# Order edges for three mixer steps, and two squares from GpSimd to VectorE, in a two-layer hybrid encoder

## The chip, the cores and the metric

The kernel runs on one core of a Trainium2 chip. The core has five engines that work side by side, each through its own queue of instructions in a fixed order: TensorE (PE, matrix multiplications and transposes), VectorE (DVE), ScalarE (ACT), GpSimd (POOL) and SyncE (SP, which starts most DMA transfers). The metric is the time of one execution on the device, in microseconds (us).

## The reference, cut to what matters

Two layers of an encoder run over 512 tokens of width 1024, in fp32, and a last RMSNorm follows. One layer:

```
xn = RMSNorm(x);  h = xn @ W_in
A: gated DeltaNet, both directions (short convolution over 5 tokens on q, k, v;
   per chunk the inverse of a unit triangular matrix; scan over the chunks)
B: differential attention (two softmax maps per head, rotary)
C: attention in a window of +-128 tokens, grouped heads (rotary)
D: mLSTM, both directions (decay and input gates, running maximum)
x = x + (sum_b sigmoid(xn @ W_gate_b) * (mixer_b @ W_branch_b)) @ W_out
x = x + relu(RMSNorm(x) @ W1)^2 @ W2
```

The convolution of mixer A is `silu(centred_dwconv(qkv, conv_w))`. The output of mixer D is, per head, `num / max(|den|, exp(-m))`, summed over the two directions, then normed per head and gated.

## The kernel before

**Dense work.** A large matmul in fp32 is made of three passes in the faster fp32r format. Weight and activation are each split into a high and a low half (`wh`, `wl`; `xh`, `xl`), and high x high, low x high and high x low are summed in PSUM. The weight split is in `emit_split`: ACT copies the raw fp32 weight to `wh` (L312), DVE subtracts `wh` from it to give `wl` (L313), in two pieces for each load. Raw weights lie in two buffers (`wr`), the halves in three each. The dense matmuls form a list of items, in the order of the string `ORDER` (Aq, Ak, Av: the columns of mixer A; z, do: gates; dv, dqk: columns of D; B, C: columns of B and C) and after them branch projections, merge, output projection and MLP. An item asks for its weights with `get`, which first traces the splits up to one load ahead (two in the MLP) and the DMA some loads ahead.

**Mixers.** The mixers are generators. Each step that is traced ends with a `yield` of some nanoseconds, and `fill` then traces dense steps of about 1300 ns each until this time is paid. So dense work and mixer work are traced interleaved. The code does not fix the order on an engine: a planner puts the traced instructions into each engine's queue, by when it reckons them ready and by the order in which they were traced. An instruction traced later may so run earlier.

**The places that the change touches.**
- Mixer A, `group` (L1267 on): for each pair of heads and half of the chunks the matrix `tt_` is computed (L1287 to L1289), rounded to fp16 (`th`, L1291) and transposed on PE (L1298). DVE multiplies the transposes with a sign mask to give `D` (L1300), and POOL makes `Y` in the same way (L1301). Six levels follow that double the block size of the inverse; each begins with `th` x `D` on PE (L1311). There are 16 D in the run, in pairs.
- Mixer A, `conv`: ACT copies a PSUM bank to `ci` (L978) and scales it (L980), DVE adds the four other taps (L982), ACT and DVE finish with L984 and L986.
- Mixer D, `hout(h)`: for each of four token tiles PE sums both directions (L1475). ACT and DVE compute the denominators (L1477 to L1479). ACT scales one direction into `ho` (L1481), DVE adds the other (L1482). After the last head `head_norm` squares on POOL (L1153), sums on DVE (L1155), takes the root (L247, L248) and multiplies (L1157, L1158); PE then transposes the result (L1164).
- Mixer B, `put_k`: after the rotary product (L1028 to L1031, the last on POOL) two pieces of a key are cast on ACT (L1045, L1046), their low halves taken on DVE (L1047) and copied (L1048).
- MLP, `m1_evac(fg, j)`: for the first group of the hidden layer ACT takes the ReLU of a PSUM bank (L785) and squares it to `hh` (L786), POOL squares it again in fp32 (L787), DVE subtracts to get `hl` (L788). It runs for j = 0 to 3 in each layer. In the groups after it POOL also adds weight blocks for a seven-product scheme (L833), and PE multiplies with the splits of these (L856 to L858).

Of the kernel before, what the change touches and what calls it, by code (L numbers as in the profile page):

```python
# [13 lines left out]
AF = mybir.ActivationFunctionType  # L14
ALU = mybir.AluOpType
# [3 lines left out]
S = 512  # L19
# [96 lines left out]
def encoder(ctx: ExitStack, tc: tile.TileContext, a: dict, out: bass.AP, dbg: dict = None):  # L116
    nc = tc.nc
    dbg = dbg or {}
    pe, dve, act, pool = nc.tensor, nc.vector, nc.scalar, nc.gpsimd
    mm = pe.matmul  # L120
    cp = ctx.enter_context(tc.tile_pool(name="cp", bufs=1))
    lp = ctx.enter_context(tc.tile_pool(name="lp", bufs=1))
    wp = ctx.enter_context(tc.tile_pool(name="wp", bufs=3))
# [10 lines left out]
    def nm(s):  # L134
        cnt[0] += 1
        return f"{s}_{cnt[0]}"
# [11 lines left out]
    def A(dt=F32, s="t", w=S):  # L148
        o = place(s)
        return ar.tile([P, 576], dt, tag="ar", name=nm(s))[:, o:o + w]  # L150

    def AH(s="h"):
        t = ar.tile([P, 1152], F16, tag="ar", name=nm(s))[:, 2 * place(s):]
        return t[:, :S], t[:, S:2 * S]
# [5 lines left out]
    def B4(dt=F32, s="b", off=None):  # L160
        return B(dt, s, off=off).rearrange("p (k c) -> p k c", k=4)
# [4 lines left out]
    def PSM(dt=F32):  # L166
        return pm.tile([P, S], dt, tag="pm", name=nm("pm"))

    def SM(w, tag):
        return sp.tile([P, w], F32, tag=tag, name=nm(tag))  # L170

    def f(ap):
        return ap.bitcast(F32)

    v4 = lambda ap: ap.rearrange("p (d h c) -> p d h c", d=2, h=2)
# [7 lines left out]
    def bmid(ap2, n):  # L183
        sh = list(ap2.shape)
        return ap2.unsqueeze(1).to_broadcast([sh[0], n] + sh[1:])

    def rev(ap, r):
        return ap[:, ::-1] if r else ap
# [113 lines left out]
    def emit_split(i):  # L302
        w = loads[i]
        raw = w["src"]() if "src" in w else raws.pop(i)
        if "dest" in w:
            wh, wl = w["dest"]()
        else:
            wh = wp.tile([P, w["kt"], w["nc"]], F32R, tag="wh", name=nm("wh"))
            wl = wp.tile([P, w["kt"], w["nc"]], F32R, tag="wl", name=nm("wl"))
        n = w["kt"] // G["sp"]  # L310
        for k in range(0, w["kt"], n):
            act.copy(wh[:, k:k + n], raw[:, k:k + n])  # L312
            dve.tensor_tensor(wl[:, k:k + n], raw[:, k:k + n], f(wh[:, k:k + n]), op=ALU.subtract)  # L313
        wt[i] = (wh, wl)

    def step():
# [227 lines left out]
    def build(l, L):  # L544
# [234 lines left out]
        def m1_evac(fg, j):  # L779
            def ev(ps):  # L780
                if j == 0:
                    L.h[fg] = (B4(F32R, "hh"), B4(F32R, "hl"))
                hh, hl = L.h[fg]
                r, q = A(s="r"), A(s="r2")
                act.activation(r, ps, AF.Relu)  # L785
                act.activation(hh[:, j, :], r, AF.Square)  # L786
                pool.tensor_tensor(q, r, r, op=ALU.mult)  # L787
                dve.tensor_tensor(hl[:, j, :], q, f(hh[:, j, :]), op=ALU.subtract)  # L788
            return ev

# [175 lines left out]
    def conv(L, kind, h, ps):  # L966
        if kind == "k" and h == 0:
            L.kb, L.ss = B4(s="kb"), None
        if kind == "q" and h == 0:
            L.qb = B4(s="qb")  # L970
        if kind == "v" and h == 0:
            L.vb = B4(s="vb")
        ft = {"q": 0, "k": 4, "v": 8}[kind] + h
        cw = L.cw
        ci = A(s="ci", w=S + 4)
        pool.memset(ci[:, 0:2], 0.0)
        pool.memset(ci[:, S + 2:S + 4], 0.0)
        act.copy(ci[:, 2:S + 2], ps)  # L978
        ac = A(s="ac")
        act.activation(ac, ci[:, 0:S], AF.Copy, scale=cw[:, 0, ft:ft + 1])  # L980
        for k in range(1, 5):
            dve.scalar_tensor_tensor(ac, ci[:, k:k + S], cw[:, k, ft:ft + 1], ac, op0=ALU.mult, op1=ALU.add)  # L982
        sg = A(s="sg")
        act.activation(sg, ac, AF.Tanh)  # L984
        dst = {"q": L.qb if kind == "q" else None, "k": L.kb, "v": L.vb if kind == "v" else None}[kind][:, h, :]
        dve.scalar_tensor_tensor(dst, sg, 1.0, ac, op0=ALU.add, op1=ALU.mult)  # L986
# [55 lines left out]
    def put_k(rt, dh, dl, h0, l0):  # L1042
        for e, (own, oth) in enumerate(halves):
            t, u = dh[:, h0 + e, :], dl[:, l0 + e, :]
            act.copy(t[own], rt[own])  # L1045
            act.copy(t[oth], rt[own])  # L1046
            dve.tensor_tensor(u[own], rt[own], f(t[own]), op=ALU.subtract)  # L1047
            dve.tensor_copy(u[oth], f(u[own]))  # L1048

    def b_qk(L, hp, kind, b, bank):  # L1050
        if kind == "q" and b == 0:
# [94 lines left out]
    def ynew():  # L1146
        return B4(F32R, "yh"), B4(F32R, "yl")
# [24 lines left out]
    def mixer_a(l, L):  # L1172
# [94 lines left out]
        def group(hp, first, cks, step, kk, kq):  # L1267
# [6 lines left out]
            for which in range(2):  # L1274
                r = PSM()
# [17 lines left out]
            sm = lambda lv: rev(sgn[:, lv], first).unsqueeze(2).to_broadcast([P, 2, 2, P])  # L1293
            smT = lambda lv: rev(sgn[:, lv], 1 - first).unsqueeze(2).to_broadcast([P, 2, 2, P])
            yield
            ps = PSM(F16)
            for m in range(4):
                pe.transpose(ps[:, blk(m)], th[:, blk(m)], identh)  # L1298
            D, Y = AH("DY")
            dve.tensor_tensor(v4(D), v4(ps), sm(0), op=ALU.mult)  # L1300
            pool.tensor_tensor(v4(Y), v4(th), smT(0), op=ALU.mult)  # L1301
            yield
            for lv in range(1, NLVL):
                w = 1 << lv
                hv = lambda t: t.rearrange("p (i g c) -> p i g c", i=2, c=w)
# [24 lines left out]
            q = A(s="q")  # L1330
# [130 lines left out]
    def mixer_d(l, L):  # L1461
        vx, EM, mb = L.vx, L.EM, L.mb
        qs, kh, kl = [[t[:, h, :] for h in range(4)] for t in (L.dq, L.dkh, L.dkl)]
        hsum = [A(s="hs") for _ in range(NT)]
        Ws = {}

        def hout(h):
            W = Ws.pop(h)
            for t in range(NT):
                hb = PSM()  # L1470
                hv = hb.rearrange("p (d c) -> p d c", d=2)
                for d in range(2):
                    js = range(0, t + 1) if d == 0 else range(t, NT)
                    for j in js:
                        mm(hv[:, d, 0:130], W[d][j][:, blk(t)], vx[:, j, h, :], start=(j == js[0]), stop=(j == js[-1]))  # L1475
                dn = SM(2, "dn")
                act.activation(dn, hv[:, :, 128], AF.Abs)  # L1477
                dve.tensor_tensor(dn, dn, EM[:, t, h::4], op=ALU.max)
                dve.reciprocal(dn, dn)  # L1479
                ho = hsum[t][:, blk(h)]  # L1480
                act.activation(ho, hv[:, 0, 0:128], AF.Copy, scale=dn[:, 0:1])  # L1481
                dve.scalar_tensor_tensor(ho, hv[:, 1, 0:128], dn[:, 1:2], ho, op0=ALU.mult, op1=ALU.add)  # L1482
                yield G['dh']

        for h in range(4):
            R, Rm = [], []
            for d in range(2):
                r = PSM()
                mm(r, oneh(0, d * 4 + h), L.RB1, start=True, stop=True)
                r1, r2 = A(s="R"), A(s="Rm")  # L1490
                act.copy(r1, r)
                dve.tensor_tensor(m4(r2), m4(r), bmid(f(neg[1][:, d, :]), 4), op=ALU.add)
                R.append(r1)
                Rm.append(r2)
            yield G['dr']
            W = [[None] * 4, [None] * 4]
            if h > 0:
                yield from hout(h - 1)
            for j in range(NT):
                s_ = PSM()  # L1500
                mm(s_, kh[h][:, blk(j)], qs[h], start=True, stop=False)
                mm(s_, kl[h][:, blk(j)], qs[h], start=False, stop=True)
                for d in range(2):
                    ts_ = range(j, NT) if d == 0 else range(0, j + 1)
                    n = len(ts_)
                    w_ = A(s="W") if n > 0 else None
                    for t in ts_:
                        act.activation(w_[:, blk(t)], (Rm if t == j else R)[d][:, blk(t)], AF.Exp,
                                       bias=mb[:, d, j, t, h:h + 1])
                    sl = slice(ts_[0] * P, (ts_[-1] + 1) * P)  # L1510
                    dve.tensor_tensor(w_[:, sl], s_[:, sl], w_[:, sl], op=ALU.mult)
                    W[d][j] = w_
                yield G['ds']
            Ws[h] = W
        yield G['hl']
        yield from hout(3)
        yT = ynew()
        L.y["d"] = yT
        ys = {}
        for tt in range(NT):  # L1520
            ys[tt] = head_norm(hsum[tt], 4, L.og[:, tt, :].rearrange("p (h c) -> p h c", h=4))
            dump_y(f"yd{l}", ys[tt], 4, tt, 0)
            yield G['yn']
        yield G['yw']
        for tt in range(NT):
            y_T(ys.pop(tt), 4, tt, 0, yT)
            yield G['yt']
        marks.add(f"yd{l}")
# [231 lines left out]
```

## Time and profile before

| | |
|---|---|
| three runs | 2319.26, 2322.42, 2322.50 us; median 2322.42 |
| the profiled execution | 2320.51 us, span of its instructions 2318.7 us |
| mean granted clock of TensorE | 0.995 |
| instructions in the profile | 41278 |
| DMA | 200.81 MB, mean 87 GB/s |

The span is the time from the first to the last instruction in the profile; the execution's own time lies around it. The clock is given as a share of TensorE's full speed (2.4 GHz). In the rows below, a line such as L313 is the line of the kernel that the instruction comes from, `wl<-wr,wh` says what it writes and reads, and `x2` that two instructions in a row are shown as one. Times are counted from the span's start.

### The profile page before, as it was taken

The numbers are of one execution on the slowest core, as the hardware profiler recorded it, in microseconds if no ns is written. First come the engines' busy times: TensorE is split into PE (matmuls) and PEld (weight loads), VectorE is DVE, ScalarE is ACT, GpSimd is POOL, SyncE is SP. The second block draws the span as 40 slices with busy tenths as digits, with TensorE's granted clock in tenths as the row PEclk, the third lists the DMA queues.
The fourth block names the chain that finished last, engine by engine and source line by source line (L and its number), as shares of the span: only waits on it lengthen the run. The fifth ranks groups of instructions, "written<-read, shape, count | busy, mean of one in ns | idle before, by whom it ended". The sixth has DMA issues, their size and how long they took to land.

```text
span 2318.7 us, 41278 instructions
## 1 busy us (share of the span) xinstructions
PE 2244.4 (97%) x15944; PEld 2010.0 (87%) x15944; DVE 1606.3 (69%) x2944; ACT 1236.3 (53%) x2827; POOL 772.9 (33%) x819
## 2 busy tenths in 40 slices
PE   7999999999999999999999999999999999999998
PEld 6879987878788989999987799878877889899998
DVE  5875547697886477677767755487877854867776
ACT  4565444765765264444445654366576633544443
POOL 1046552032332134443201655412313310434341
PEclk9999999999999999999999999999999999999999
DMA  6322131222122523233323122311322234233322
GB/s 154 93 54 65 56 96 57 58 91 82 52 72 82 164 67 125 92 102 117 110 78 91 55 56 65 92 56 55 100 74 64 65 112 139 87 100 110 101 83 91
DMA packets 234773, 200.81 MB, mean 87 GB/s; under 512 B 31825, under 2 KB 223697, under 8 KB 234577
## 3 DMA queue, kind: packets, MB, share of 16 engines
q1 hardware_dynamic: 231552, 193.09, 27.6%
q10 hardware_dynamic: 2304, 4.20, 0.5%
q8 instruction: 125, 2.05, 0.4%
q0 software_dynamic: 720, 0.89, 0.2%
q14 instruction: 72, 0.58, 0.1%
HBM read 190.25 MB, written 8.39 MB: 86 GB/s over the span
## 4 chain that ended last, share of the span: by engine, by line
PE 77%; DVE 7%; ACT 6%; POOL 4%; issue 3%; DMA 0%; POOLq 0%; DVEq 0%; ACTq 0%
PE pd L455 8%; PE pd L457 8%; PE pd L456 8%; PE pd L412 7%; PE pd L413 7%; PE pd L414 7%; PE pm L858 4%; PE pm L857 4%; PE pm L856 4%; PE pd L427 2%; PE pd L426 2%; PE pd L428 2%; ACT r L1028 1%; POOL r L1031 1%; DVE wl L313 1%
## 5 line engine op out<-in xcount | busy, mean ns | idle before, releaser
L313 DVE TENSOR_TENSOR wl<-wr,wh 128x512 fp32r<-128x512 f32 x540 | 413.1, 785 | 168.0 <-ACT wh L312 160.6
L312 ACT CAST wh<-wr 128x512 fp32r<-128x512 f32 x540 | 316.6, 620 | 216.0 <-PE pd L456 76.9
L455 PE MATMUL pd<-xh,wh 128*128 128x512 f32 (+1 forms) x768 | 307.5, 401 | 0.5 <-ACT xh L242 0.5
L457 PE MATMUL pd<-xh,wl 128*128 128x512 f32 (+1 forms) x768 | 298.0, 388 | 0.0
L456 PE MATMUL pd<-xl,wh 128*128 128x512 f32 (+1 forms) x768 | 296.0, 386 | 1.8 <-DVE xl L243 1.8
L414 PE MATMUL pd<-wh,hl 128*128 128x256 f32 x896 | 247.4, 276 | 0.0
L413 PE MATMUL pd<-wl,hh 128*128 128x256 f32 x896 | 247.4, 276 | 0.0
L412 PE MATMUL pd<-wh,hh 128*128 128x256 f32 x896 | 247.4, 276 | 0.0
L312 ACT CAST wh<-wq 128x512 fp32r<-128x512 f32 x196 | 115.2, 619 | 217.2 <-PE pd L414 91.5
L313 DVE TENSOR_TENSOR wl<-wq,wh 128x512 fp32r<-128x512 f32 x196 | 182.3, 964 | 12.9 <-ACT wh L312 12.8
L833 POOL TENSOR_TENSOR wq<-wq,wq 128x512 f32<-128x512 f32 x84 | 124.9, 1494 | 159.6 <-DVE wl L313 149.5
L457 PEld LDWEIGHTS pd<-xh,wl 128*128 128x128 f32 x768 | 145.9, 190 | 28.9
L456 PEld LDWEIGHTS pd<-xl,wh 128*128 128x128 f32 x768 | 146.5, 191 | 25.3 <-DVE xl L243 2.7
L412 PEld LDWEIGHTS pd<-wh,hh 128*128 128x128 f32 x896 | 168.2, 188 | 0.0
L413 PEld LDWEIGHTS pd<-wl,hh 128*128 128x128 f32 x896 | 168.2, 188 | 0.0
L414 PEld LDWEIGHTS pd<-wh,hl 128*128 128x128 f32 x896 | 168.2, 188 | 0.0
L455 PEld LDWEIGHTS pd<-xh,wh 128*128 128x128 f32 x768 | 146.2, 191 | 22.2 <-ACT xh L242 1.0
L701 DVE TENSOR_TENSOR x<-pd,x 128x512 f32<-128x512 f32 x124 | 84.8, 688 | 95.9 <-PE pd L414 95.9
L412 PE MATMUL pd<-wh,xh 128*128 128x256 f32 x512 | 150.8, 295 | 0.0
L413 PE MATMUL pd<-wl,xh 128*128 128x256 f32 x512 | 145.6, 284 | 0.0
L414 PE MATMUL pd<-wh,xl 128*128 128x256 f32 x512 | 144.7, 283 | 0.0
L1031 POOL TENSOR_TENSOR r<-r,r 128x512 f32<-128x512 f32 x26 | 36.1, 1389 | 299.8 <-DVE r L1030 217.1
(394 smaller groups left out, 6635.0 us busy)
## 6 DMA issues: line engine op xcount, KB each, us to landing
wr<-in_w_in SPq DMA_DIRECT2D x92, 512.0 KB
wr<-in_w_mlp SPq DMA_DIRECT2D x72, 512.0 KB
wr<-in_w_gate SPq DMA_DIRECT2D x64, 512.0 KB
wq<-in_w_mlp SPq DMA_DIRECT2D x56, 512.0 KB
wr<-in_w_branch SPq DMA_DIRECT2D x32, 512.0 KB
wr<-in_w_out SPq DMA_DIRECT2D x16, 512.0 KB
x<-in_x SPq DMA_DIRECT2D x16, 256.0 KB
gsd<-gs ACTq DMA_DIRECT2D x16, 256.0 KB
```

The source lines that it names most:

```text
L312: act.copy(wh[:, k:k + n], raw[:, k:k + n])
L313: dve.tensor_tensor(wl[:, k:k + n], raw[:, k:k + n], f(wh[:, k:k + n]), op=ALU.subtract)
L412: mm(o, th, wh[:, k4, :], start=(kt == 0 and tt % 2 == 0), stop=False)
L413: mm(o, th, wl[:, k4, :], start=False, stop=False)
L414: mm(o, tl, wh[:, k4, :], start=False, stop=(kt == kts - 1 and tt % 2 == 1))
L455: mm(o, w1_, xh[kt][:, sl], start=(kt == 0 and hi_ == 0), stop=False)
L456: mm(o, w1_, xl[kt][:, sl], start=False, stop=False)
L457: mm(o, w2_, xh[kt][:, sl], start=False, stop=last)
L833: pool.tensor_tensor(d[:, k:k + 2], x[:, k:k + 2], y[:, k:k + 2], op=op)
L856: mm(o, w1_, xh[k], start=(k == 0 and b == 0), stop=False)
L857: mm(o, w1_, xl[k], start=False, stop=False)
L858: mm(o, w2_, xh[k], start=False, stop=(k == 3 and b == 1))
```

## The change

Two helpers are new. `lead(i)` notes an instruction as the latest leader of its engine. `behind(i)` adds an order edge from that leader to an instruction that is traced later on the same engine. The edge fixes the order in the queue only, and carries no semaphore. Leaders are D of mixer A (DVE) and the two instructions that make `ho` in mixer D (ACT and DVE). Placed behind the leaders are the weight splits (ACT and DVE), the convolution's taps (DVE) and the keys' casts of mixer B and C (ACT and DVE). Apart from this, the third and fourth square of `m1_evac` go from POOL to DVE.

```diff
+    last = {}
+    nosync = mybir.DependencyInfo(mybir.DependencyClass.NoSync, mybir.DependencyReason.DATA)
+
+    def lead(i):
+        last[i.ins.engine] = i.ins.name
+        return i
+
+    def behind(i):
+        if i.ins.engine in last:
+            tc.add_manual_dep(i.ins, last[i.ins.engine], nosync, reason="dense work behind the mixer's step")
+        return i
...
-            act.copy(wh[:, k:k + n], raw[:, k:k + n])
-            dve.tensor_tensor(wl[:, k:k + n], raw[:, k:k + n], f(wh[:, k:k + n]), op=ALU.subtract)
+            behind(act.copy(wh[:, k:k + n], raw[:, k:k + n]))
+            behind(dve.tensor_tensor(wl[:, k:k + n], raw[:, k:k + n], f(wh[:, k:k + n]), op=ALU.subtract))
...
-                pool.tensor_tensor(q, r, r, op=ALU.mult)
+                (pool if j < 2 else dve).tensor_tensor(q, r, r, op=ALU.mult)
...
-            dve.scalar_tensor_tensor(ac, ci[:, k:k + S], cw[:, k, ft:ft + 1], ac, op0=ALU.mult, op1=ALU.add)
+            behind(dve.scalar_tensor_tensor(ac, ci[:, k:k + S], cw[:, k, ft:ft + 1], ac, op0=ALU.mult, op1=ALU.add))
...
-            act.copy(t[own], rt[own])
-            act.copy(t[oth], rt[own])
-            dve.tensor_tensor(u[own], rt[own], f(t[own]), op=ALU.subtract)
-            dve.tensor_copy(u[oth], f(u[own]))
+            behind(act.copy(t[own], rt[own]))
+            behind(act.copy(t[oth], rt[own]))
+            behind(dve.tensor_tensor(u[own], rt[own], f(t[own]), op=ALU.subtract))
+            behind(dve.tensor_copy(u[oth], f(u[own])))
...
-            dve.tensor_tensor(v4(D), v4(ps), sm(0), op=ALU.mult)
+            lead(dve.tensor_tensor(v4(D), v4(ps), sm(0), op=ALU.mult))
...
-                act.activation(ho, hv[:, 0, 0:128], AF.Copy, scale=dn[:, 0:1])
-                dve.scalar_tensor_tensor(ho, hv[:, 1, 0:128], dn[:, 1:2], ho, op0=ALU.mult, op1=ALU.add)
+                lead(act.activation(ho, hv[:, 0, 0:128], AF.Copy, scale=dn[:, 0:1]))
+                lead(dve.scalar_tensor_tensor(ho, hv[:, 1, 0:128], dn[:, 1:2], ho, op0=ALU.mult, op1=ALU.add))
```

## Rows read from the trace of the kernel before

**Rows 1.** The page's first part: busy time, share of the span, instructions of each engine.
```profile
PE 2244.4 (97%) x15944; PEld 2010.0 (87%) x15944; DVE 1606.3 (69%) x2944; ACT 1236.3 (53%) x2827; POOL 772.9 (33%) x819
```
**Rows 2.** PE's waits: line and what it waited for, us in total, times, longest.
```profile
PE pm L1164 <- DVE hv L247: 10.5, 4, 3.6
PE pm L1311 <- DVE DY L1300: 6.3, 2, 3.2
PE pm L858 <- DVE wl L313: 5.8, 2, 2.9
```
**Rows 3.** Stretches: length, busy us of PE, PEld, DVE, ACT, POOL; PE's clock; DMA.
```profile
116.00:174.00 58.00, 54.63 (x400) 43.84 (x399) 41.65 (x64) 39.17 (x92) 27.59 (x43) 0.97 0.25 54
174.00:464.00 290.00, 283.82 (x2275) 247.97 (x2274) 177.10 (x324) 159.75 (x409) 121.16 (x135) 1.00 0.22 66
```
**Rows 4.** The same view of two short stretches, behind a wait of PE each.
```profile
154.20:158.10 3.90, 3.90 (x37) 3.62 (x37) 3.29 (x6) 1.28 (x4) 3.90 (x8) 0.59 0.46 134
861.40:864.70 3.30, 3.30 (x18) 3.30 (x17) 3.30 (x4) 1.02 (x2) 2.87 (x2) 0.51 0.00 0
```
**Rows 5.** Timeline of POOL, 846 to 866: start, duration, instruction, idle time before it.
```profile
848.72 4.09 POOL L833 TENSOR_TENSOR wq<-wq,wq 128x512 f32<-128x512 f32 x1 [5.98 <-DVE wl L313]
...
856.76 2.04 POOL L787 TENSOR_TENSOR r<-r 128x512 f32<-128x512 f32 x2
```
**Rows 6.** Timeline of DVE, 846 to 866.
```profile
849.77 1.88 DVE L243 TENSOR_TENSOR xsl<-xf,xsh 128x512 fp32r<-128x512 f32 x3
857.83 1.51 DVE L788 TENSOR_TENSOR hl<-r,hh 128x512 fp32r<-128x512 f32 x1 [6.18 <-POOL r L787]
859.27 1.28 DVE L313 TENSOR_TENSOR wl<-wq,wh 128x512 fp32r<-128x512 f32 x2
860.47 0.68 DVE L788 TENSOR_TENSOR hl<-r,hh 128x512 fp32r<-128x512 f32 x1
861.07 4.65 DVE L313 TENSOR_TENSOR wl<-wq,wh 128x512 fp32r<-128x512 f32 x4
```
**Rows 7.** Timeline of ACT, 846 to 866.
```profile
852.55 0.63 ACT L786 ACTIVATE hh<-r 128x512 fp32r<-128x512 f32 x1
```
**Rows 8.** Timeline of PE, 856 to 861.5.
```profile
860.00 0.38 PE L858 MATMUL pm<-xh,wl 128*128 128x256 f32 x1 [2.89 <-DVE wl L313]
```
**Rows 9.** Timeline of DVE, 120 to 156.
```profile
121.67 1.29 DVE L313 TENSOR_TENSOR wl<-wr,wh 128x512 fp32r<-128x512 f32 x2 [3.97 <-PE pm L1216]
...
145.66 0.88 DVE L313 TENSOR_TENSOR wl<-wr,wh 128x512 fp32r<-128x512 f32 x1 [2.25 <-ACT wh L312]
146.46 4.24 DVE L982 SCALAR_TENSOR_TENSOR ac<-ci,cw,ac 128x512 f32<-128x512 f32 x3
...
151.64 1.09 DVE L982 SCALAR_TENSOR_TENSOR ac<-ci,cw,ac 128x512 f32<-128x512 f32 x1
152.66 1.09 DVE L313 TENSOR_TENSOR wl<-wr,wh 128x512 fp32r<-128x512 f32 x1
153.67 0.41 DVE L1300 TENSOR_TENSOR DY<-pm,c_sgn 128x512 f16<-128x512 f16 x1
```
**Rows 10.** Timeline of PE, 140 to 156.
```profile
141.56 0.40 PE L428 MATMUL pd<-xh,wl 128*128 128x512 f32 x1
...
144.38 0.40 PE L1298 MATMUL pm<-c_identh,th 128*128 128x128 f16 x4
144.62 0.61 PE L1246 MATMUL pm<-c_ident,kb 128*128 128x128 f32 x4
144.98 0.48 PE L428 MATMUL pd<-xh,wl 128*128 128x512 f32 x1
```
**Rows 11.** Timeline of DVE, 463 to 477.
```profile
471.94 1.49 DVE L1157 TENSOR_TENSOR sq<-hs,hr 128x512 f32<-128x512 f32 x1
```
**Rows 12.** Timeline of ACT, 463 to 477.
```profile
467.16 0.62 ACT L1045 CAST bkh<-r 64x512 fp32r<-64x512 f32 x1 [1.98 <-POOL r L1031]
...
469.99 0.63 ACT L1481 ACTIVATE hs<-pm,dn 128x128 f32<-128x128 f32 x2
```

## The prediction

> **What bounds the kernel now.** The busy shares come first: TensorE (PE) works 97% of the span, VectorE (DVE) 69%, ScalarE (ACT) 53% [rows 1]. So the end is set by PE, and a change that takes nothing from PE's own work can only win where PE stands still or runs slowly. The table of PE's waits says where. Besides the start of the kernel, three kinds of wait hold PE for about 3 us at a time, once in each layer: at the first level of mixer A's inverse (L1311, waiting for DVE's D of L1300), for the first head norm of mixer D (L1164, longest 3.6), and in the first MLP group (L858, waiting for the low half of a weight, L313) [rows 2]. The table of stretches shows a second price: slices of 58 us that hold such a wait have a granted clock of 0.97, against 1.00 over the 290 us from 174 [rows 3]; six slices are so, one for each of the six waits, and one at the kernel's end. Cut finer, the clock is 0.59 for 3.9 us behind the first wait and 0.51 for 3.3 us behind the third [rows 4]: 2.4 GHz falls to 1.2 GHz once PE has stood for 3 us. At that clock 0.41 × 3.9 = 1.6 and 0.49 × 3.3 = 1.6 us are lost, so each wait costs its length and 1.6 us more. All six together: 2 × (3.2 + 3.6 + 2.9) + 6 × 1.6 = 29 us, the most that the change can bring.
>
> The sum is made against the profiled execution, 2320.5 us (span 2318.7 and 1.8 around it). The median of the three runs lies 1.9 us above it; the stated time adds that.
>
> **Part 1, two squares to DVE.** In the first MLP group POOL squares four activations (L787) one after the other with its weight sums (L833). The last two squares come at 856.76, behind four sums that began at 848.72 [rows 5]. DVE's difference of L788 waits 6.18 us for the first of them, and the two splits of the weight that PE is about to want stand behind it in DVE's queue and run at 859.27 [rows 6]. Their inputs were there long before: ACT's second squared high half ends at 853.18 [rows 7]. PE goes on at 860.00 after 2.89 us [rows 8]. With both squares on DVE, its queue gets two instructions of 0.68 us more (the length of the undisturbed L788 of this shape [rows 6]), and the 6.18 us of idle hide them: 851.65 (end of the L243s at 849.77), then two squares, two L788 and two L313, six of 0.68, give 855.7 even if nothing is ready before; with ACT's 853.18 + 3 × 0.68 as the other bound, 855.2. PE's need was at 857.1. The wait goes, and with it the slow clock: 2.89 + 1.6 = 4.5 us in each layer, 9.0 in both. Next late would be the following splits (L313 from 861.07), which move up with DVE, since 859.27 becomes 854 to 855; POOL is rid of 2.04 us.
>
> The row that speaks against this: the first L833 took 4.09 us, while the other three share 856.76 − 852.81 = 3.95, 1.3 each; it ran until 1.2 us after DVE ended its unbroken run of splits at 851.65 [rows 5, 6]. And L788 took 1.51 beside POOL's square, four splits 4.65 beside two POOL sums [rows 6]. So a DVE operation on two SBUF operands and POOL's take turns. The Trainium skill says the same as a rule (SBUF — State Buffer, section "Who interferes with whom"): a VectorE instruction with two SBUF inputs and a GpSimd instruction that reads SBUF share a port pair by an exclusive lock, the second blocks until the first is through. By that rule alone the six DVE operations could each wait for a sum; the rows agree with it, and no row shows six in turn.
>
> Bounds of the part, from rows: nothing in turn, −9.0; each of six DVE operations waiting 1.3 for a POOL sum, of which there are only four: 851.65 + 6 × 0.68 + 4 × 1.3 = 860.9 for the last split, against 860.55 before, with the first split at about 858.9 against 859.9: about 1 us gained a layer, −2, and the clock still lost. The work between lies nearer to the first, as the sums that run before 853 hold back only squares that have slack. I take −9.0.
>
> **Part 2, D of mixer A ahead of dense work on DVE (L1300).** In front of D at 153.67 stand, from 145.66, three splits (0.88, and two of 1.09) and four convolution steps of L982 (4.24 and 1.09) [rows 9], though D's transposes ended on PE by 144.8 [rows 10]. By the order in which the code is traced, the splits come later than D and the convolutions of that item (Av1) earlier. So the edges put behind D only splits, eight in each layer: the three, and five that ran before, among them the two at 121.67 [rows 9], whose halves PE takes from 141.56 [rows 10], before D can exist. That is the added wait. Behind the held splits stands the next DMA too, since only two raw buffers exist; its data are wanted more than 10 us later.
>
> Where the planner puts D first: D's two instructions run from 144.3 to 145.3, the held split ends at 145.3 + 0.7 = 146.0, and PE stands from 141.56. It can bring forward the mixer's transposes in that stretch, two L1246 of 0.36 and two L1298 of 0.24 by the distance of their starts, 1.2 us [rows 10]. That leaves 4.4 − 1.2 = 3.2 us, the size of the wait that goes [rows 2]; the slow clock stays. With DVE freed of the held splits before 143, the transposes may come some 0.5 us earlier: I take −0.5 a layer, −1. The other bound is full closure, −(3.2 + 1.6) = −4.8 a layer; the loss on the other side is the first rival below. The other three pairs of D in a layer hold back two splits each, which PE takes 13 us or more later: nothing.
>
> **Part 3, the sums of mixer D (L1481, L1482).** The long wait of L1164 starts from the fourth head's last outputs. The head norm's product L1157 runs on DVE at 471.94 [rows 11], behind keys of mixer B (L1047, L1048) and behind L1482, which itself waited for ACT's L1481 at 469.99; this stood behind four casts of keys that began at 467.16 after waiting 1.98 us for POOL [rows 12]. The edges put a key's casts behind the sums of the tiles traced before it. But these keys are traced between the second tile's sum and the third's, so only the second's (0.35 us) passes them; the third and fourth stay behind, and L1157 has no edge at all. I take −0.5 a layer, −1; bounds: the whole wait and its clock, −(3.6 + 1.6) = −5.2, and +1.3, a pair of splits like that at 121.67 [rows 9] which these edges push into the wait. Elsewhere, by the same reading of the code's order beside the trace, sums hold back splits that PE wants 6 to 14 us later.
>
> **Sum.** 2320.5 − 9.0 − 1 − 1 = 2309.5; with the 1.9 of the median 2311.
>
> **Rivals.**
> A. *D stays behind the convolutions, and PE starves.* The edges remove only splits from in front of D. If the planner leaves the four L982 there, they take 4.24 + 1.0 us from 145.66 on, to 150.9 [rows 9], D's pair ends at 151.6, the split that PE needs from 141.56 at 152.3. PE stands 10.7 − 1.2 = 9.5 us in place of 3.2: +6.3 a layer, +12.6. With the squares, 2320.5 − 9.0 + 12.6 = 2324.1, stated 2326: slower than before. It decides from the end of D's pair: past 145.3 the first group is a loss, past 145.3 + 4.5 = 149.8 it eats all that the squares bring. For it: the convolutions are traced first, and they stand ahead of D now. Against: POOL works beside them and makes them long here, which need not hold in another order, and PE's own order can change too. Chance 0.25.
> B. *All three waits close*: 2320.5 − 29 = 2291.5, stated 2293. For it: D and the fourth head's sums each wait on DVE only by queue order, and the planner lays out the whole order anew. Against: Av3's low half and L1157. Chance 0.10.
> C. *DVE and POOL take turns in the MLP group*, so the wait of L858 shrinks by 1 us only: 2320.5 − 2 − 2 = 2316.5, stated 2318. For and against stand in part 1. Chance 0.10.
> D. *The edges do nothing*: where the planner already has an order that meets them, or moves dense splits without any effect on PE. Only the squares count: 2313. Against: eight splits that must move. Chance 0.10.
>
> **How the numbers follow.** The forecast has the other 0.45, with a range of its own of 2303 to 2317: −5 a layer where one more wait shrinks, +3 where the first group's wait grows. The whole range takes in most of A (2314 to 2332 around its 2326) and half of B: 2298 to 2327. About 0.2% of this time, 4.6 us, is what a measurement can tell from no change, so faster means under 2317.8, slower over 2327. Faster: the forecast 0.43, B 0.10, D 0.09, a third of C 0.03: 0.65. Slower: 0.11 of A and 0.01 of the forecast: 0.12. The rest, 0.23, is the same.
>
> **What would show it.** Part 1: no wait of L858 on L313 above 0.5 us, two DVE squares between 849 and 855, clock 1.00 in the slices of the MLP's start. It is wrong if L313 still ends after 857 there. Part 2: no split between the transposes L1298 and D; a new wait of PE for a low half (L428 on L313) before D, about as long as the old one on L1300; rival A shows it at 9 us. Part 3: the wait of L1164 still about 3 us, with L1157 late behind L1482. The forecast is wrong altogether if the waits of L1300 and L1164 are both gone, or if PE waits over 6 us for a split that an edge held.

## The result: slower, by 17 us

| | us |
|---|---|
| before, median | 2322.43 |
| after, median of four runs | 2339.62 (2337.83 to 2340.59) |
| after against before, ratio | 1.0076, 95% interval 1.0065 to 1.0088 |
| the profiled execution after, and its span | 2337.83, 2336.1 |

The time lies outside the forecast range, and on the other side of no change. One execution of the kernel before, of 9881 us, stands beside experiments 5 to 8 and is left out of every median. The lines of the kernel after stand 11 lower in its code (L1300 is L1311, L1164 is L1175, L858 is L869, L313 is L324).

The page of the kernel after: busy time, share of the span, instructions. The engines do the same work as before [rows 1].

```profile
PE 2247.6 (96%) x15944; PEld 2009.5 (86%) x15944; DVE 1608.2 (69%) x2948; ACT 1237.5 (53%) x2827; POOL 772.3 (33%) x815
```

PE's waits in the kernel after: line and what it waited for, total, times, longest.

```profile
PE pm L1175 <- DVE sq L1169: 17.8, 10, 4.1
...
PE pm L1322 <- DVE DY L1311: 12.1, 2, 6.0
PE pm L869 <- DVE wl L324: 4.1, 4, 1.3
...
PE pd L439 <- DVE wl L324: 3.0, 2, 1.5
...
PE pm L1175 <- DVE hv L258: 3.2, 2, 1.6
```

The wait for D has doubled (6.3 in all before [rows 2]), and a wait for a weight's low half stands beside it. The head norm's waits (the two rows of L1175) went from 15.6 us (10.5 [rows 2] and 5.1 for sq) to 21.0. Of the three long waits only that of the MLP's first group has shrunk: from 2.9 us in each layer to two shorter ones, 2.0 together, the longest 1.3.

Stretches of the kernel after: length, busy us of PE, PEld, DVE, ACT, POOL, then PE's clock.

```profile
116.00:174.00 58.00, 49.65 (x346) 38.24 (x346) 40.25 (x61) 36.66 (x87) 25.70 (x42) 0.91 0.20 43
150.00:155.00 5.00, 3.06 (x27) 2.16 (x27) 4.97 (x9) 2.02 (x4) 5.00 (x9) 0.50 0.07 6
155.00:160.00 5.00, 5.00 (x25) 3.67 (x23) 5.00 (x7) 2.15 (x6) 3.87 (x8) 0.67 0.41 119
464.00:522.00 58.00, 50.97 (x294) 43.47 (x295) 48.35 (x100) 37.83 (x83) 16.28 (x14) 0.94 0.28 91
812.00:870.00 58.00, 55.33 (x419) 51.09 (x418) 44.70 (x67) 33.70 (x69) 17.57 (x12) 1.00 0.28 82
```

The clock of mixer A's slice fell from 0.97 [rows 3] to 0.91, that of the head norm's from 0.97 to 0.94, and that of the MLP's start rose from 0.97 to 1.00. Where the dense matmuls of both traces are lined up one by one, the loss is made at two places in each layer: 5.9 us (layer 0) and 6.2 us (layer 1) in the first group of mixer A, 4.3 and 4.6 us around mixer D's head norm. The MLP's start gives back 2.4 us each time, about what its wait and its slow clock make: 2.9 + 1.6 - 2.0 = 2.5. The sum, 21.0 - 4.8 = 16.2, leaves 1.2 of the span's 17.4 us for all that lies between.

**The first group.** DVE's timeline in the kernel after:

```profile
145.14 4.90 DVE L993 SCALAR_TENSOR_TENSOR ac<-ci,cw,ac 128x512 f32<-128x512 f32 x4 [2.96 <-ACT ac L991]
149.96 0.74 DVE L1311 TENSOR_TENSOR DY<-pm,c_sgn 128x512 f16<-128x512 f16 x2
150.73 0.87 DVE L997 SCALAR_TENSOR_TENSOR vb<-sg,ac 128x512 f32<-128x512 f32 x1
151.52 2.11 DVE L324 TENSOR_TENSOR wl<-wr,wh 128x512 fp32r<-128x512 f32 x2
```

And PE's:

```profile
142.50 0.92 PE L1309 MATMUL pm<-c_identh,th 128*128 128x128 f16 x8 [0.34 <-ACT th L1302]
150.42 0.73 PE L1322 MATMUL pm<-DY,th 128*128 128x64 f16 x8 [6.05 <-DVE DY L1311]
152.67 0.79 PE L439 MATMUL pd<-xh,wl 128*128 128x512 f32 x1 [1.51 <-DVE wl L324]
```

No split stands in front of D any more; those from 121.67 on [rows 9] come after it. But the four taps do, though D's input was there at 143.42, when DVE stood idle for the taps' input: the engine takes its queue in order. The two splits at 151.52 are the ones that ran at 121.67 before. PE stands 6.05 and 1.51 us in place of 3.17, 4.4 more. Behind it the clock costs 0.50 × 3.06 + 0.33 × 5.00 = 3.2 us of PE's busy time in the two stretches shown, 1.6 more than before; together 6.0, the loss of this place.

**The head norm.** A weight whose split ACT ran early in the kernel before, and the first matmul with it:

```profile
452.55 1.13 ACT L312 CAST wh<-wr 128x512 fp32r<-128x512 f32 x2
467.14 0.28 PE L412 MATMUL pd<-wh,xh 128*128 128x256 f32 x1
```

The same weight in the kernel after, and what PE waits for in front of it:

```profile
475.73 1.14 ACT L323 CAST wh<-wr 128x512 fp32r<-128x512 f32 x2
477.45 0.45 PE L1175 MATMUL pm<-c_ident,sq 128*128 128x128 f32 x1 [4.09 <-DVE sq L1169]
477.55 0.78 PE L423 MATMUL pd<-wh,xh 128*128 128x256 f32 x2
```

The split that ended 13.5 us before PE took the weight now ends after PE has run out of dense work; what PE has next, the head norm's transposes, is not ready before 477.45. Between the dense matmuls that stand at 450 and 522 in the kernel before, PE stands 2.4 us longer (2.7 at the same place of layer 1), and the slow clock takes 0.7 us more (1.3). The rest of the loss there, 1.2 and 0.6 us, is not accounted for.

### The profile page after: what moved, and what is told of

Its sections match the earlier page's. It is cut to its first block, busy times and chain, and to the rows that moved or that the text cites. A ratio compares the mean times of both kernels' runs of the same rounds, so it can differ in the third digit from the quotient of the medians.

```text
span 2336.1 us, 41266 instructions
## 1 busy us (share of the span) xinstructions
PE 2247.6 (96%) x15944; PEld 2009.5 (86%) x15944; DVE 1608.2 (69%) x2948; ACT 1237.5 (53%) x2827; POOL 772.3 (33%) x815
## 5 line engine op out<-in xcount | busy, mean ns | idle before, releaser
L324 DVE TENSOR_TENSOR wl<-wr,wh 128x512 fp32r<-128x512 f32 x540 | 406.4, 773 | 142.3 <-ACT wh L323 138.7
L324 DVE TENSOR_TENSOR wl<-wq,wh 128x512 fp32r<-128x512 f32 x196 | 187.0, 988 | 12.8 <-ACT wh L323 12.7
L424 PE MATMUL pd<-wl,xh 128*128 128x256 f32 x512 | 145.3, 284 | 0.6 <-DVE wl L324 0.6
```

The lines of the kernel that those rows point to most:

```text
L324: behind(dve.tensor_tensor(wl[:, k:k + n], raw[:, k:k + n], f(wh[:, k:k + n]), op=ALU.subtract))
L424: mm(o, th, wl[:, k4, :], start=False, stop=False)
```

## The experiments

All are against the kernel before on the same chip, with its median there in brackets. A run's ratio is given with its 95% interval. None leaves any work out.

**1 to 3. The three parts alone.** Squares: the kernel before with

```diff
-                pool.tensor_tensor(q, r, r, op=ALU.mult)
+                (pool if j < 2 else dve).tensor_tensor(q, r, r, op=ALU.mult)
```

> The kernel before with the third and fourth square of m1_evac on DVE, and no order edges. Theory 1 (the squares win a part of the wait of L858, because DVE and POOL take turns): 2316 to 2318, about 5 us faster than before in both layers together, with a wait of L858 of about 1.3 us left. Theory 2 (the squares win nothing by themselves, the smaller wait in the changed kernel comes from the new order): 2322, as before. Theory 3, as the prediction had it: 2313.

Edges of D: the kernel after with the squares on POOL, and

```diff
-                lead(act.activation(ho, hv[:, 0, 0:128], AF.Copy, scale=dn[:, 0:1]))
-                lead(dve.scalar_tensor_tensor(ho, hv[:, 1, 0:128], dn[:, 1:2], ho, op0=ALU.mult, op1=ALU.add))
+                act.activation(ho, hv[:, 0, 0:128], AF.Copy, scale=dn[:, 0:1])
+                dve.scalar_tensor_tensor(ho, hv[:, 1, 0:128], dn[:, 1:2], ho, op0=ALU.mult, op1=ALU.add)
```

> Only the edges behind D of mixer A, none behind the sums of mixer D, squares on POOL as before. Theory 1 (in the first group D stays behind four convolution taps, and PE starves for the low half that the edge holds back): about 6 us lost in each layer, 2334 to 2335, with the wait of L1311 near 6 us and one of 1.5 us for a low half behind it, everything after that as before. Theory 2 (the loss there comes only together with the other edges): 2322 to 2325.

Edges of mixer D's sums: the kernel after with the squares on POOL, and

```diff
-            lead(dve.tensor_tensor(v4(D), v4(ps), sm(0), op=ALU.mult))
+            dve.tensor_tensor(v4(D), v4(ps), sm(0), op=ALU.mult)
```

> Only the edges behind the sums of mixer D (L1481, L1482), none behind D of mixer A, squares on POOL as before. Theory 1 (these edges give PE less dense work ahead of the head norm, so that it stands earlier and longer): about 4.5 us lost in each layer, 2331 to 2332, the first group of mixer A as before. Theory 2 (the loss at the head norm is carried over from the first group of mixer A): 2321 to 2324.

| | us (2321.60) | ratio |
|---|---|---|
| squares alone | 2317.55 | 0.9982 (0.9973 to 0.9990) |
| D's edges alone | 2333.34 | 1.0047 (1.0033 to 1.0061) |
| the sums' edges alone | 2331.30 | 1.0038 (1.0025 to 1.0050) |

-4.05, +11.74 and +9.70 us add to 17.4; all together lost 17.2. Theory 1 holds three times (D's edges end 0.7 us under its range, far above that of theory 2): the parts add up, and each loses or wins at its own place.

**4. The squares on ACT.**

```diff
-                pool.tensor_tensor(q, r, r, op=ALU.mult)
+                if j < 2:
+                    pool.tensor_tensor(q, r, r, op=ALU.mult)
+                else:
+                    act.activation(q, r, AF.Square)
```

> No edges; the third and fourth square of m1_evac on ACT instead of POOL (kernel before) or DVE (kernel after). ACT idles there and shares nothing with POOL in the rows seen so far. Theory 1 (DVE and POOL take turns, which keeps a part of the wait of L858): with ACT the six DVE operations become four, the wait falls under 1 us, 2313 to 2316, faster than the squares on DVE. Theory 2 (turns do not matter, the queue order does): the same time as with the squares on DVE within 1 us.

2316.05 us (2321.60), ratio 0.9978 (0.9969 to 0.9987). The median is 1.5 us below that of the squares on DVE and at the edge of theory 1's range; the intervals overlap, so the times alone do not part the theories. The timelines do. DVE with the squares on DVE (start, duration, instruction):

```profile
851.91 0.68 DVE L787 TENSOR_TENSOR r<-r 128x512 f32<-128x512 f32 x1
852.69 1.60 DVE L788 TENSOR_TENSOR hl<-r,hh 128x512 fp32r<-128x512 f32 x1
854.22 1.78 DVE L313 TENSOR_TENSOR wl<-wq,wh 128x512 fp32r<-128x512 f32 x1
855.92 1.78 DVE L787 TENSOR_TENSOR r<-r 128x512 f32<-128x512 f32 x1
857.62 1.76 DVE L313 TENSOR_TENSOR wl<-wq,wh 128x512 fp32r<-128x512 f32 x1
859.31 0.68 DVE L788 TENSOR_TENSOR hl<-r,hh 128x512 fp32r<-128x512 f32 x1
```

POOL's four sums beside them:

```profile
849.05 9.78 POOL L833 TENSOR_TENSOR wq<-wq,wq 128x512 f32<-128x512 f32 x4 [5.97 <-DVE wl L313]
```

DVE with the squares on ACT:

```profile
853.13 0.68 DVE L791 TENSOR_TENSOR hl<-r,hh 128x512 fp32r<-128x512 f32 x1
853.73 1.28 DVE L313 TENSOR_TENSOR wl<-wq,wh 128x512 fp32r<-128x512 f32 x2
855.31 1.41 DVE L791 TENSOR_TENSOR hl<-r,hh 128x512 fp32r<-128x512 f32 x1 [0.29 <-ACT r L790]
```

Four of the six DVE operations take 1.6 to 1.8 us in place of 0.68 while POOL adds: DVE and POOL take turns. With the squares on ACT the two splits are done at 855.0 and the wait of 2.9 us falls to one of 0.7; with them on DVE a wait of 1.3 us stays. Taking turns is what follows from the rule that the prediction weighed (the Trainium skill, SBUF — State Buffer, "Who interferes with whom"), and the trace agrees with it here: 1.6 to 1.8 us in place of 0.68. Who pays is also a matter of gaps. As long as DVE's operations follow each other without one, each takes 0.68 us and POOL's first sum pays: begun at 849.05 (squares on DVE) and 850.28 (on ACT) it takes 4.70 and 5.89 us, and ends 1.2 us after DVE's unbroken run, which goes to 852.59 and 855.02. On DVE the run breaks off where L788 waits for its square, and the two begin to alternate there; with the squares on ACT both splits still lie in the run.

**5 and 6. D ahead of the taps.** Both trace the taps of convolution Av1 (and what follows them) nine dense steps later; number 5 with the edges of D, number 6 without any edge. In number 6 D is L1306, the taps are L983, and Q, the first product of each level, which begins from an identity that POOL copies (L1314), is L1318.

```diff
+        if kind == "v" and h == 1:
+            pend.append([9, taps])
+        else:
+            taps()
```

> Edges behind D of mixer A only, as in the run that lost 11.7 us with them; in addition the taps of the convolution Av1 are traced nine dense steps later, so that they too stand behind D. Theory 1 (what costs is D's place behind four taps, by which the held low half of Av3 comes at 151.5): D comes 6 us earlier, PE's waits in the first group shrink from 7.5 to 1 to 3 us, 2318 to 2323. Theory 2 (holding back the eight splits costs by itself, wherever D stands): 2330 to 2334, PE still waits 5 us or more there.

> The kernel before without any edge, only the taps of Av1 traced nine dense steps later; the planner then puts D in front of them and of the splits, and no split is held. Theory 1 (the wait of L1311 is the taps' place in DVE's queue, nothing else): that wait closes with its slow clock, about 4.8 us in each layer, 2311 to 2314. Theory 2 (the four taps and the splits only move, and PE waits for them a few us later): 2320 to 2323.

With the edges 2330.09 us (2321.91), 1.0033 (1.0021 to 1.0045); without 2325.62, 1.0015 (1.0006 to 1.0024). D does come early in both, at 143.0 and 143.1, and theory 1 fails in both. Theory 2 has the time of number 5; that of number 6 lies 2.6 us above the range of its theory 2. DVE's timeline in number 6:

```profile
143.13 0.95 DVE L1306 TENSOR_TENSOR DY<-pm,c_sgn 128x512 f16<-128x512 f16 x2 [0.86 <-PE pm L1304]
145.16 1.37 DVE L983 SCALAR_TENSOR_TENSOR ac<-ci,cw,ac 128x512 f32<-128x512 f32 x1 [1.07 <-ACT ac L980]
148.13 0.98 DVE L1318 TENSOR_TENSOR Q<-pm,c_sgn 128x256 f16<-128x256 f32 x2 [1.60 <-POOL Q L1314]
149.03 5.88 DVE L983 SCALAR_TENSOR_TENSOR ac<-ci,cw,ac 128x512 f32<-128x512 f32 x6
154.82 1.09 DVE L313 TENSOR_TENSOR wl<-wr,wh 128x512 fp32r<-128x512 f32 x1
155.84 1.09 DVE L983 SCALAR_TENSOR_TENSOR ac<-ci,cw,ac 128x512 f32<-128x512 f32 x1
156.86 2.11 DVE L313 TENSOR_TENSOR wl<-wr,wh 128x512 fp32r<-128x512 f32 x2
158.89 0.68 DVE L987 SCALAR_TENSOR_TENSOR vb<-sg,ac 128x512 f32<-128x512 f32 x1
159.49 0.74 DVE L1318 TENSOR_TENSOR Q<-pm,c_sgn 128x256 f16<-128x256 f32 x2
```

PE's waits for it:

```profile
148.61 0.28 PE L1323 MATMUL pm<-Q,DY 128*128 128x64 f16 x4 [1.77 <-DVE Q L1318]
...
159.96 0.29 PE L1323 MATMUL pm<-Q,DY 128*128 128x64 f16 x4 [3.15 <-DVE Q L1318]
```

The wait for D is gone, and waits of 1.8 and 3.2 us stand at the next two Q: the first waits for POOL's identity copies, then the taps and splits that D has passed stand in front of the second. Together they are longer than the wait for D was (4.9 us against 3.2). From 149 to 160 DVE is never idle. So D's place alone is not what the first group waits for; what is left is the work that DVE and POOL have to do over several links, which experiments 10 and 11 make less.

**7 and 8. The sums' edges by halves.** Number 7 has `lead` at L1492 and L1493 and `behind` at the keys' casts only, number 8 at the weight splits only (both keep it at the convolution's taps).

> Edges behind the sums of mixer D only, and only for the keys' casts of mixer B (put_k); weight splits are free. Theory 1 (what costs is the held splits, which take dense work away from in front of the head norm; the keys' edges do what they are for): the wait of L1164 shrinks by 1 to 3 us in each layer, 2314 to 2320. Theory 2 (the keys' edges cost as well): 2325 or more.

> Edges behind the sums of mixer D only, and only for the weight splits (and the taps, of which none runs there); the keys' casts are free. Theory 1 (the held splits cost): 2329 to 2335, at least what all of these edges together lost (9.7 us). Theory 2 (the splits have 6 to 14 us of slack and cost nothing, the keys' order does it): 2320 to 2324.

Keys 2324.15 us (2321.91), 1.0010 (1.0001 to 1.0019); splits 2330.20, 1.0033 (1.0021 to 1.0044). The splits carry most of the loss, +8.3, in the range of their theory 1 but less than the 9.7 that it names; the keys add 2.2, a time between the ranges of their two theories. The timeline of ACT in number 8:

```profile
466.87 0.62 ACT L1056 CAST bkh<-r 64x512 fp32r<-64x512 f32 x1 [2.55 <-POOL r L1042]
467.39 0.36 ACT L1492 ACTIVATE hs<-pm,dn 128x128 f32<-128x128 f32 x1
467.77 0.62 ACT L1057 CAST bkh<-r 64x512 fp32r<-64x512 f32 x1
468.40 0.62 ACT L1056 CAST bkh<-r 64x512 fp32r<-64x512 f32 x1
469.04 0.62 ACT L1057 CAST bkh<-r 64x512 fp32r<-64x512 f32 x1
469.68 1.14 ACT L323 CAST wh<-wr 128x512 fp32r<-128x512 f32 x2
```

And of PE:

```profile
470.36 0.79 PE L423 MATMUL pd<-wh,xh 128*128 128x256 f32 x2 [3.34 <-ACT wh L323]
472.67 0.58 PE L424 MATMUL pd<-wl,xh 128*128 128x256 f32 x1 [1.52 <-DVE wl L324]
```

The split at 469.68 ran at 452.55 in the kernel before. The sum in front of it, L1492 at 467.39, stands itself behind a cast that waits 2.55 us for POOL, and three more casts follow; PE, which took the weight at 467.14 before, stands 3.34 and 1.52 us for it. The keys' edges do part of what they say, and it does not pay. PE in number 7:

```profile
473.13 0.63 PE L1175 MATMUL pm<-c_ident,sq 128*128 128x128 f32 x4 [2.45 <-DVE sq L1169]
476.96 0.63 PE L1175 MATMUL pm<-c_ident,sq 128*128 128x128 f32 x4 [0.41 <-ACT wh L323]
480.12 0.63 PE L1175 MATMUL pm<-c_ident,sq 128*128 128x128 f32 x4 [1.16 <-DVE sq L1169]
```

The long wait falls from 3.64 to 2.45 us, and the slice's clock rises to 1.00. But the second and third tile, which did not wait before, now wait 0.41 and 1.16, and 1.43 more comes at L1570: theory 1's 1 to 3 us are won at the first tile and more than given back behind it.

**9. D's edges with Av3's splits free.** As D's edges alone, but the two splits of Av3's weight have no edge.

```diff
+            hold = (lambda x: x) if av3(i) else behind
-            behind(act.copy(wh[:, k:k + n], raw[:, k:k + n]))
+            hold(act.copy(wh[:, k:k + n], raw[:, k:k + n]))
...
```

The split on DVE changes in the same way; `av3(i)` is true for the load of Av3's weight.

> Edges behind D of mixer A only, but not for the two splits of Av3's weight, which PE takes from 141 to 148; six splits in each layer stay held, and D stays behind four taps. Theory 1 (PE starves for Av3's low half): with Av3's 24 matmuls to do, 5.5 us, PE reaches the first level later, its waits in the first group shrink from 7.5 to 2 to 4 us, 2321 to 2326. Theory 2 (the held half is not it, the planner's other order in the first group costs): 2331 to 2334.

2324.75 us (2320.62), 1.0018 (1.0009 to 1.0026): +4.1 in place of +11.7, as theory 1 had it. D stands at 149.87, behind the same four taps; PE waits 2.2 us for it and 1.6 for a low half of z0. Two held splits of eight make two thirds of the loss.

**10 to 12. Less work of POOL beside the taps, and a better kernel.** Q's identity copied by ACT; Y computed by DVE; the first of these with the squares on ACT.

```diff
-                pool.tensor_copy(m4(Q), bmid(identh, 4))
+                act.copy(m4(Q), bmid(identh, 4))
```

```diff
-            pool.tensor_tensor(v4(Y), v4(th), smT(0), op=ALU.mult)
+            dve.tensor_tensor(v4(Y), v4(th), smT(0), op=ALU.mult)
```

> The kernel before; the identity that each level of mixer A's inverse copies into Q (L1308, POOL, 96 copies) is copied by ACT. No edge. Theory 1 (the convolution taps and splits before D are long because POOL works beside them, 1.0 to 1.1 us in place of 0.7): the taps beside Q's copies fall to about 0.75, D comes 1 to 1.5 us earlier, the wait of L1311 falls to 1.5 to 2.5 us and may not slow the clock: 2313 to 2320. Theory 2 (the taps are long for another reason, or ACT becomes late): 2321 or more.

> The kernel before; Y of mixer A (L1301, two of 1.6 us on POOL in the first group) goes to DVE, where an operation of this shape takes 0.41 us, behind D. No edge. Theory 1 (the first two taps take 1.66 and 1.54 us because they take turns with Y on POOL): they fall to about 0.75, D comes some 1.5 us earlier, the wait of L1311 shrinks to about 1.5 us and its slow clock goes: 2313 to 2319. Theory 2 (what DVE saves in turns it pays for Y, 0.8 us behind D): 2320 to 2324.

> The squares of m1_evac with j = 2 and 3 on ACT, and Q's identity copies on ACT, no edge. If both gains add: 5.5 us for the squares and what the copies alone give, 2308 to 2315. If the copies alone lose, it stands that much above 2316.

| | us (2320.62) | ratio |
|---|---|---|
| Q on ACT | 2318.03 | 0.9991 (0.9982 to 1.0000) |
| Y on DVE | 2319.45 | 0.9995 (0.9986 to 1.0004) |
| Q and two squares on ACT | 2312.08 | 0.9967 (0.9954 to 0.9979) |

With Q on ACT the tap and the splits in front of D fall to 0.7 us (1.09 before [rows 9]), D's wait to 1.8 us, as theory 1 said; DVE's timeline there:

```profile
150.75 0.68 DVE L313 TENSOR_TENSOR wl<-wr,wh 128x512 fp32r<-128x512 f32 x1
151.35 0.75 DVE L982 SCALAR_TENSOR_TENSOR ac<-ci,cw,ac 128x512 f32<-128x512 f32 x1
152.01 0.68 DVE L313 TENSOR_TENSOR wl<-wr,wh 128x512 fp32r<-128x512 f32 x1
152.62 0.41 DVE L1300 TENSOR_TENSOR DY<-pm,c_sgn 128x512 f16<-128x512 f16 x1
```

The median is 2.6 us lower, with an interval that touches no change. With Y on DVE the first three taps take 3.12 us in place of 4.24 [rows 9] and D's wait is 2.1 us, but the time is not told from no change and lies between the two theories. Both moves to ACT together are the best kernel of the study, 8.5 us faster than the kernel before; the two gains alone, 5.5 and 2.6, make 8.1.

## Why the prediction was wrong, step by step

**The forecast's sum.** 2309.5 us was forecast for the profiled execution, which took 2337.8. Of the 28.3 us between, part 1 makes 4.9, part 2 12.7 and part 3 10.7.

**The bound and the price of a wait.** The bound was right: PE's work did not change, and the first group and the MLP's start lost or won what PE stood there and what the clock took behind it. The price of 1.6 us for the slow clock, the same for every wait, was not. For the first group after it was too small: a second wait of 1.5 us falls into the slow stretch, which takes 3.2 us, as worked out above. For the MLP's wait it was too sure: that wait of 2.9 us stands unchanged in nine more profiles, and in half of all cases no slow clock follows it (last section), so "2.4 GHz falls to 1.2 GHz once PE has stood for 3 us" is what two waits did and no rule.

**Part 1, the squares.** The direction was right, the size wrong: -9.0 taken, -4.1 measured alone. The step that failed is "the sums that run before 853 hold back only squares that have slack": POOL's sums run until 858.8, as each also waits for DVE, and the second split follows the second square and ends at 859.4, not at 855.7. Rival C had the mechanism, but its price of -2 is half of what was measured: it left the slow clock in place, and that went (1.00 in the slice of the MLP's start).

**Part 2, D.** -1 taken, +11.7 measured. The step that failed is "Where the planner puts D first: D's two instructions run from 144.3 to 145.3": the planner left the four taps ahead, and D ran from 149.96. The fork was drawn rightly, and the wrong branch was held for the likelier. Rival A has place, order and cause: the taps stay, D's pair ends at 150.7 (151.6 estimated), PE starves for Av3's low half. That its price, +12.6, is within 1 us of the run is luck in part: PE waits 7.6 us, not 9.5, and the clock, for which it took nothing more, takes 1.6 more. What the prediction did not see is that even its good branch gains nothing: with D early, the wait moves to the levels behind it (experiments 5 and 6).

**Part 3, the sums.** -0.5 a layer taken, within bounds of -5.2 and +1.3; +9.7 measured in both, 4.9 a layer, outside them. The step that failed is the upper bound, "a pair of splits like that at 121.67 [rows 9] which these edges push into the wait", and with it "sums hold back splits that PE wants 6 to 14 us later". PE wanted the weight of the split at 452.55 14.6 us later, at 467.14. But the sum that now stands in front of this split ran at 467.69 before, later than that need, so no slack is left; and the casts around that sum, one of which waits 2.55 us for POOL, put it off further. PE is then out of dense work, and it stands: 3.34 and 1.52 us at the weight itself in number 8, 4.1 us at the head norm's transposes in the kernel after. No rival put this at mixer D.

**Rival A's sum.** Rival A's 2324.1 with the squares at -4.1 and the sums' edges at +9.7 would have been 2320.5 - 4.1 + 12.6 + 9.7 = 2338.7, against 2337.8 of the profiled execution: of the 13.7 us by which rival A itself fell short, part 3 makes 9.7.

**What is left open.** Why D's edges still lose 8.2 us where D is early (experiment 5), against 3.7 without edges, stays open in the main. The edges, and with them the held splits, are the one difference, and by the dense matmuls most of it lies in the first groups: 4.7 and 3.3 us lost in the two layers against 2.4 and 2.3. PE's waits there do not make it up: with the edges 5.2 and 3.5 us for Q and 0.6 in each layer for a low half, without them 4.9 and 5.0 for Q.

## What to carry to other kernels

An order edge that holds back prefetch work spends the slack of a later stage: count it from the place where the held work will really stand, behind everything that its leader waits for, to where the bounding engine needs it. A reordering can move the wait of a chain of dependent steps to its next link, as here (experiment 6); less work on the engine beside the chain shortened it (3.2 to 1.8 us, experiment 10), with a gain at the edge of what these runs can tell. If two engines take turns, look for a third: with POOL's squares on ACT a wait of 0.7 us was left, on DVE 1.3, though the two times are not told apart.

## What the runs showed of the hardware

The length of PE's wait did not settle its clock. The wait of 2.9 us in the MLP's first group stands in both layers of ten profiles (before, and experiments 2, 3 and 5 to 11). In ten of these twenty cases the clock fell from 2.4 to 1.2 GHz behind it, as in [rows 4], and in ten it stayed at 1.00; experiments 2, 5, 8 and 11 have one layer of each kind. So it stayed, behind a wait of 2.88 us that ended at 859.10, with Q on ACT:

```profile
859.50:872.00 12.50, 11.86 (x104) 11.67 (x104) 11.22 (x14) 4.48 (x8) 7.11 (x5) 1.00 0.33 109
```

In the same run it fell behind a wait of 1.8 us in layer 1 (0.72 from 1297 to 1303) and not behind the same wait in layer 0; behind 2.45 us it stayed at 1.00 (experiment 7). No run was made to show what decides it. A price of a slow clock taken from one profile is therefore a price that is paid only in some of the cases.

With work in both queues DVE and POOL both pay: four operations of DVE in a row took 1.6 to 1.8 us in place of 0.68, and POOL's four sums 9.8 us, where three took 1.3 each beside an idle DVE [rows 5]. While DVE's operations follow without a gap, POOL's sum alone pays: its first one ended 1.2 us behind DVE's unbroken run in the kernel before [rows 5, 6] and in experiments 1 and 4.
